# Order of work on VectorE and GpSimd in the attention loop of a two-layer decoder step

## The chip, the cores and the metric

One core of one Trainium2 chip runs the whole program. The metric is the device time of one execution in microseconds. Before the change the median of three runs is 1964.24 us (1963.74 to 1965.5).

The engines are named as the profile names them: PE (TensorE, with PEld for its weight loads), DVE (VectorE), ACT (ScalarE), POOL (GpSimd) and SP (SyncE, which issues most of the transfers).

## The reference

Two layers over 1024 prompt tokens and 8 sample tokens, model width 1024, all in float32. Layer 0 mixes with a gated recurrent block, layer 1 with sliding-window attention; a squared-ReLU MLP follows each. The change is inside the attention of layer 1, for the prompt tokens:

```python
def sink_attention(q, k, v, dist, mask, sinks):
    s = jnp.einsum('...qkgd,...skd->...kgqs', q, k).astype(jnp.float32) * (HEAD_DIM ** -0.5)
    s = s - alibi_slopes()[:, :, None, None] * dist.astype(jnp.float32)
    s = jnp.where(mask, s, NEG_INF)
    sink = sinks.astype(jnp.float32).reshape(N_KV, GROUP)[:, :, None, None]
    m = jnp.maximum(jnp.max(s, axis=-1, keepdims=True), sink)
    e = jnp.exp(s - m)
    p = e / (jnp.sum(e, axis=-1, keepdims=True) + jnp.exp(sink - m))
    return jnp.einsum('...kgqs,...skd->...qkgd', p.astype(v.dtype), v)
```

Queries come in 8 blocks of 128; each block sees its own block of keys and the one before it, and of these exactly 128 keys per query (window 128). There are 16 heads of width 64, in 4 groups that share keys and values.

## The kernel before, in words

The attention loop runs over 32 steps `g`: four groups of four heads (a pair of query tiles `t`, `t + 1`) times 8 query blocks `b`. Every query has 128 valid keys out of 256, and the kernel packs them into one 128-wide row: for key column j it takes the score of the older block or of the newer one, whichever is in the window. A step has three stages.

- `stage_a(g)` makes the probabilities. TensorE makes scores against both key blocks into a two-bank PSUM tile `bSS` (L1031), of which there is one. GpSimd meanwhile writes the distance bias into the step's `se` slot (L1034, L1036). VectorE then copies, under a mask, the older block's scores over the newer ones (L1038, only where there is an older block, so 28 times), adds the bias (L1039, the sum), takes the maximum (L1040) and a scaled negative of it (L1041). ScalarE takes four exponentials with row sums (L1044), VectorE the reciprocals (L1046), GpSimd scales by them (L1048).
- `stage_b(g)` transposes the four probability blocks on TensorE into the PSUM tile `bT` (L1058), of which there is one bank. ScalarE copies the result into the right half of `pt` (L1060), VectorE multiplies it by the mask of the newer block into the left half (L1062, the mask product). GpSimd subtracts the newer block's values from the older block's (L1056, the value difference) into one of four slots `dvs`.
- `stage_c(g0)` serves two steps at once. For each of them it multiplies values by the ScalarE half of `pt`, then value differences by the VectorE half (L1078, into the one bank `bO`), so that the mix of both value blocks comes out; ScalarE and VectorE split the result into two parts (L1085, L1086), and it is stored to DRAM (L1089) or kept.

In step `g` of the loop the scores of step g + 2, the transposes of step g and, every second time, the products of steps g - 2 and g - 1 are emitted. Between them TensorE gets matmuls of other work: first the query projections of the later heads (L938, with their own followers on ScalarE and VectorE: squares L877, a rounded part L879 and the remainder L880, and the transfers of both on SyncE, L886 and L887), and from step 22 on the output projection (L244), which needs the attention outputs loaded back (L1183) and the weights `w_out` (loaded by SyncE, L177, split by ScalarE L183 and VectorE L184). Each pair of query tiles has factors from its norms (L893 to L908, with L310 to L315), which bias, maximum and exponentials of the group need.

What sets the order: TensorE's instructions stay in the order in which they are written, because `pinned()` ties each to the one before it. On the other engines a scheduler of the framework orders the instructions when the program is built, by what is ready in its own estimate and by priority, which is the order of emission unless `tc.high_priority()` raises it. The order that comes out is a fixed queue for each engine: on the chip an instruction that waits holds everything behind it on that engine.

Of the kernel before, what the change touches and what calls it, by code (L numbers as in the profile page):

```python
# [13 lines left out]
ALU = mybir.AluOpType  # L14
PSUM = bass.MemoryType.PSUM

P = 128
# [9 lines left out]
NB = SEQ // P  # L27
# [38 lines left out]
def trunk(ctx: ExitStack, tc: tile.TileContext, I, O):  # L66
    nc = tc.nc
    pe, act, dve, pool, sp = nc.tensor, nc.scalar, nc.vector, nc.gpsimd, nc.sync
# [39 lines left out]
    def W(s="w"):  # L108
        return wp.tile([P, T], F32, tag="W", name=nm(s))
# [8 lines left out]
    def B(tag=None):  # L118
        if tag is None:
            tag = ring[turn[0] % len(ring)]  # L120
            turn[0] += 1
        return psum["pool"].tile([P, 512], F32, tag=tag, bufs=BANKS[tag], name=nm("b" + tag))


    def SB():
        return psum["pool"].tile([P, 1024], F32, tag="SS", bufs=1, name=nm("bSS"))
# [13 lines left out]
    def r_(x):  # L140
        return x.bitcast(F32R)
# [687 lines left out]
    def attention(hs):  # L829
# [123 lines left out]
        def vblk(b, p):  # L953
            h = b // 4
            o = (b % 4) * 256 + p * P
            return v_tiles[h][:, o:o + P]
# [34 lines left out]
        newer, newer_t = side_of[:, 0:P], side_of[:, P:2 * P]  # L991
        se2 = [W("se"), W("se")]
        ses = [x[:, o:o + 516].rearrange("p (x k) -> p x k", x=4) for x, o in ((se2[0], 0), (se2[0], 516), (se2[1], 0))]
        dvs = [se2[1][:, 516 + o:516 + o + P] for o in range(0, 4 * P, P)]
# [8 lines left out]
        def four(x):  # L1003
            return x.unsqueeze(1).to_broadcast([P, 4, P])

        def by_head(x):
            return x.rearrange("p (u t) -> p u t", u=2)
# [12 lines left out]
        def stage_a(g):  # L1020
            t, b = STEPS[g]
            p, i = divmod(t, 4)
            se, dn, s = ses[g % 3], den[g % 3], SB()
            f = fac[:, t % 4:t % 4 + 2, :, b, :]
            f0, f1 = [f[:, :, n, :].rearrange("p t u -> p u t") for n in range(2)]
            old, new = [s.rearrange("p (x h k) -> p x h k", x=4, h=2)[:, :, n, :] for n in range(2)]
            k0, n = ((b - 1) * P, 2 * P) if b else (0, P)
            for x in range(4):
                u, v = divmod(x, 2)
                for a, y in enumerate(kst[p][u]):  # L1030
                    pe.matmul(s[:, x * 256 + 256 - n:x * 256 + 256], lhsT=r_(qs[t + v][u][:, b * P:b * P + P]),  # L1031
                              rhs=r_(y[:, k0:k0 + n]), start=(a == 0), stop=(a == 1))
                h = (2 * p + u) * 4 + i + v
                pool.tensor_scalar(se[:, x, 0:P], dist if b else dist0, f[:, v, 1, u:u + 1], -SLOPES[h], ALU.mult, ALU.mult)  # L1034
                yield
            pool.tensor_tensor(by_head(se[:, :, P]), sinks[:, p, :, i:i + 2], f1, ALU.mult)  # L1036
            if b:
                dve.copy_predicated(new, four(newer.bitcast(mybir.dt.int32)), old)  # L1038
            dve.tensor_tensor(se[:, :, 0:P], new, se[:, :, 0:P], ALU.add)  # L1039
            dve.tensor_reduce(dn[:, 0:4], se, axis=mybir.AxisListType.X, op=ALU.max)  # L1040
            dve.scalar_tensor_tensor(by_head(dn[:, 4:8]), by_head(dn[:, 0:4]), -1.0, f0, ALU.mult, ALU.mult)  # L1041
            for x in range(4):
                u, v = divmod(x, 2)
                act.activation(se[:, x, :], se[:, x, :], AF.Exp, scale=f[:, v, 0, u:u + 1],  # L1044
                               bias=dn[:, 4 + x:5 + x], accum_out=dn[:, 8 + x:9 + x])
            dve.reciprocal(dn[:, 8:12], dn[:, 8:12])  # L1046
            for x in range(4):
                pool.tensor_scalar(se[:, x, 0:P], se[:, x, 0:P], dn[:, 8 + x:9 + x], 0.0, ALU.mult, ALU.add)  # L1048
            yield

        def stage_b(g):
            t, b = STEPS[g]
            se, pt = ses[g % 3], B("T")
            y = live["pt", g] = W("pt")
            if b:
                pool.tensor_tensor(dvs[g % 4], vblk(b - 1, t // 4), vblk(b, t // 4), ALU.subtract)  # L1056
            for x in range(4):
                pe.transpose(pt[:, x * P:x * P + P], se[:, x, 0:P], ident)  # L1058
                yield
            act.copy(y[:, 512:1024], pt)  # L1060
            if b:
                dve.tensor_tensor(y[:, 0:512].rearrange("p (x k) -> p x k", x=4), pt.rearrange("p (x k) -> p x k", x=4),  # L1062
                                  four(newer_t), ALU.mult)
            yield
# [162 lines left out]
        with pinned():  # L1227
            for g in range(AHEAD):
                ready(g)
                run(stage_a(g))  # L1230
                upto(41 + 6 * g)
        def scores(g):
            if g < NG:
                ready(g)
                run(stage_a(g))

        for g in range(NG):
            table = FILL if g < G0 else EARLY
            place = {0: 2, 1: 1}.get((g + AHEAD) % NB, 0)
            with pinned():  # L1240
                if place == 0:
                    scores(g + AHEAD)
                if g != G0:
                    upto(int(pace(table, g + 1 / 3)))
                if g and g % 2 == 0:
                    stage_c(g - 2)
                if g == G0:
                    run(fill)
                    taken[0], fill = 0, steps
                if place == 1:  # L1250
                    scores(g + AHEAD)
                upto(int(pace(table, g + 2 / 3)))
                run(stage_b(g))
                upto(int(pace(table, g + 1)))
                if place == 2:
                    scores(g + AHEAD)
# [373 lines left out]
```

## Time and profile before

| | |
|---|---|
| median of three runs | 1964.24 us (1963.74 to 1965.5) |
| the profiled execution | 1962.05 us |
| its span on the core | 1960.3 us |
| mean granted clock of TensorE | 0.996 |
| TensorE busy, whole span | 1945.4 us (99%) |
| VectorE busy, whole span | 1481.4 us (76%) |
| ScalarE busy, whole span | 1008.5 us (51%) |
| GpSimd busy, whole span | 367.8 us (19%) |
| attention loop | about 1040 to 1240 us of the span |

The span runs from the first to the last instruction of the profiled execution; its time is a little longer. A row of the timeline has the start in us, the duration in us, the engine, the line of the kernel, the operation, what is written and read, how many are merged, and in brackets the engine's idle time just before, with what ended it. A row of a window has the stretch, its length, then the busy time (and count) of PE, PEld, DVE, ACT and POOL, the granted clock, the DMA share and GB/s. "PE bSS L1031 <- DVE se L1039: 4.3, 2, 3.5" means that TensorE at line 1031 waited for VectorE's line 1039 for 4.3 us in all, twice, at most 3.5 us.

### The profile page before, as it was taken

The numbers are of one execution on the slowest core, as the hardware profiler recorded it, in microseconds if no ns is written. First come the engines' busy times: TensorE is split into PE (matmuls) and PEld (weight loads), VectorE is DVE, ScalarE is ACT, GpSimd is POOL, SyncE is SP. The second block draws the span as 40 slices with busy tenths as digits, with TensorE's granted clock in tenths as the row PEclk, the third lists the DMA queues.
The fourth block names the chain that finished last, engine by engine and source line by source line (L and its number), as shares of the span: only waits on it lengthen the run. The fifth ranks groups of instructions, "written<-read, shape, count | busy, mean of one in ns | idle before, by whom it ended". The sixth has DMA issues, their size and how long they took to land.

```text
span 1960.3 us, 34219 instructions
## 1 busy us (share of the span) xinstructions
PE 1945.4 (99%) x12844; PEld 1812.2 (92%) x12844; DVE 1481.4 (76%) x2711; ACT 1008.5 (51%) x1993; POOL 367.8 (19%) x702
## 2 busy tenths in 40 slices
PE   9999999999999999999999999999999999999999
PEld 8999999999999899999999887999999999999998
DVE  8896737987777878778743777579877779687784
ACT  6476635543434555445554676555443436455552
POOL 2330000000000232331032666000000003223321
PEclk9999999999999999999999999999999999999999
DMA  5111242244445788888452345612444447788877
GB/s 184 44 44 54 70 165 83 109 152 157 141 157 177 229 224 236 220 202 206 130 155 81 110 112 191 210 65 103 158 144 150 148 172 263 210 201 216 233 201 181
DMA packets 115909, 308.17 MB, mean 157 GB/s; under 512 B 17560, under 2 KB 46240, under 8 KB 115744
## 3 DMA queue, kind: packets, MB, share of 16 engines
q0 software_dynamic: 30720, 104.18, 22.1%
q1 hardware_dynamic: 54496, 129.36, 20.1%
q10 hardware_dynamic: 30528, 72.45, 10.3%
q8 instruction: 101, 1.65, 0.3%
q14 instruction: 64, 0.52, 0.1%
HBM read 178.08 MB, written 115.16 MB: 150 GB/s over the span
## 4 chain that ended last, share of the span: by engine, by line
PE 92%; DVE 3%; ACT 2%; DMA 1%; issue 1%; POOL 1%; SPq 0%; DVEq 0%; ACTq 0%
PE bD L609 36%; PE bZ L609 26%; PE bP L244 11%; PE bS L244 7%; PE bT L244 3%; PE bP L938 3%; PE bSS L1031 1%; PE bO L1078 1%; PE bS L968 1%; PE bT L1058 1%; DMA x<-xT 1%; ACT se L1044 0%; DVE wl L184 0%; DMA raw<-w_out 0%; DVE sq L295 0%
## 5 line engine op out<-in xcount | busy, mean ns | idle before, releaser
L609 PEld LDWEIGHTS bD<-op,op 128*128 128x128 f32 x3072 | 380.5, 188 | 7.9
L609 PE MATMUL bD<-op,op 128*128 128x260 f32 x3072 | 383.0, 282 | 0.0
L609 PEld LDWEIGHTS bD<-tl,op 128*128 128x128 f32 x2880 | 362.4, 188 | 11.6 <-DVE ho L757 0.3
L609 PE MATMUL bD<-tl,op 128*128 128x260 f32 x2880 | 366.4, 282 | 0.1
L622 POOL DMA_DIRECT2D tl<-hsum x210 | 125.4, 682 | 886.9 <-PE bD L609 785.4
L456 ACT CAST op<-ws 128x512 fp32r<-128x512 f32 (+2 forms) x288 | 158.7, 561 | 246.9 <-DVE ws L577 114.8
L609 PE MATMUL bZ<-op,op 128*128 128x512 f32 x1152 | 282.2, 394 | 0.0
L609 PE MATMUL bZ<-tl,op 128*128 128x512 f32 x1080 | 271.8, 394 | 0.2 <-DVE tl L464 0.2
L609 PEld LDWEIGHTS bZ<-op,op 128*128 128x128 f32 x1152 | 210.4, 188 | 43.6 <-ACT he L743 0.2
L609 PEld LDWEIGHTS bZ<-tl,op 128*128 128x128 f32 x1080 | 194.4, 188 | 37.7 <-DVE tl L464 0.7
L464 DVE TENSOR_TENSOR tl<-tl 128x520 fp32r<-128x520 f32 (+1 forms) x210 | 136.4, 692 | 77.1 <-ACT tl L463 76.9
L456 ACT CAST op<-raw 128x512 fp32r<-128x512 f32 (+2 forms) x216 | 120.9, 562 | 133.9 <-PE bD L609 73.0
L457 DVE TENSOR_TENSOR op<-ws,op 128x512 fp32r<-128x512 f32 (+2 forms) x288 | 171.5, 610 | 7.3 <-ACT op L456 7.1
L457 DVE TENSOR_TENSOR op<-raw,op 128x512 fp32r<-128x512 f32 (+2 forms) x216 | 131.7, 611 | 9.3 <-ACT op L456 8.5
L757 DVE TENSOR_TENSOR ho<-bD,ho 128x520 f32<-128x520 f32 x140 | 97.5, 697 | 37.1 <-PE bD L609 36.2
L463 ACT CAST tl<-tl 128x520 fp32r<-128x520 f32 (+1 forms) x210 | 117.5, 626 | 2.1 <-DVE ho L674 0.7
L184 DVE TENSOR_TENSOR wl<-raw,wh 128x512 fp32r<-128x512 f32 (+1 forms) x73 | 63.6, 890 | 34.7 <-ACT wh L183 18.1
L747 DVE TENSOR_TENSOR ho<-bZ,ho 128x512 f32<-128x512 f32 x72 | 49.6, 689 | 44.2 <-PE bZ L609 44.0
L731 ACT COPY he<-bZ 128x512 f32<-128x512 f32 x72 | 42.0, 583 | 75.3 <-PE bZ L609 69.8
L757 DVE TENSOR_TENSOR he<-bD,he 128x520 f32<-128x520 f32 x71 | 49.4, 696 | 40.6 <-PE bD L609 40.3
L749 ACT COPY he<-bZ 128x512 f32<-128x512 f32 x68 | 39.9, 587 | 77.0 <-PE bZ L609 64.9
L183 ACT CAST wh<-raw 128x512 fp32r<-128x512 f32 (+1 forms) x76 | 57.2, 775 | 36.2 <-PE bT L244 11.3
(371 smaller groups left out, 3839.4 us busy)
## 6 DMA issues: line engine op xcount, KB each, us to landing
raw<-w_up SPq DMA_DIRECT2D x64, 512.0 KB, 3.8
tl<-hsum POOLq DMA_DIRECT2D x120, 260.0 KB, 6.7
raw<-w_dn SPq DMA_DIRECT2D x64, 384.0 KB, 6.2
tl<-hsum POOLq DMA_DIRECT2D x90, 256.0 KB, 6.3
spill<-ho POOLq DMA_DIRECT2D x32, 516.0 KB, 6.9
spill<-he POOLq DMA_DIRECT2D x32, 516.0 KB, 6.3
hsum<-ts ACTq DMA_DIRECT2D x30, 520.0 KB, 4.0
hsum<-ho ACTq DMA_DIRECT2D x30, 516.0 KB, 3.5
```

The source lines that it names most:

```text
L183: act.copy(r_(hi[:, sl]), raw[:, sl])
L184: eng.tensor_tensor(r_(lo[:, sl]), raw[:, sl], hi[:, sl], ALU.subtract)
L244: pe.matmul(o, lhsT=r_(wt[:, col(k):col(k) + P]), rhs=r_(xt[:, cs(c)]), start=(k == first and a == 0), stop=(k == final and a == 2))
L456: act.copy(r_(hi), x)
L457: dve.tensor_tensor(r_(lo), x, hi, ALU.subtract)
L463: act.copy(r_(hi), lo)
L464: eng.tensor_tensor(r_(lo), lo, hi, ALU.subtract)
L609: pe.matmul(d[:, 512 * b:512 * b + c], lhsT=r_(wt[:, j * P:j * P + P]), rhs=r_(xt[:, c * b:c * b + c]), start=first and j == 0 and a == 0, ...
L622: pool.dma_start(t[:, n:2 * n], src)
L747: dve.tensor_tensor(o0, d, o[:, HP], ALU.add)
L757: last["sum"] = dve.tensor_tensor(t, inner(d), t, ALU.add).ins
L938: pe.matmul(o, lhsT=r_(wt[:, k * P:k * P + P]), rhs=r_(xt[:, cs(c)]), start=(k == 0 and a == 0), stop=(k == M8 - 1 and a == 2))
```

## The change

Two edits. In `stage_a` the masked copy and the sum are emitted with high priority. In `stage_b` the value difference is emitted behind the transposes and for the next step: step g makes the difference that step g + 1 will use, in the slot `(g + 1) % 4`. The number of value differences is the same (28), and so are all other instructions.

```diff
             pool.tensor_tensor(by_head(se[:, :, P]), sinks[:, p, :, i:i + 2], f1, ALU.mult)
-            if b:
-                dve.copy_predicated(new, four(newer.bitcast(mybir.dt.int32)), old)
-            dve.tensor_tensor(se[:, :, 0:P], new, se[:, :, 0:P], ALU.add)
+            with tc.high_priority():
+                if b:
+                    dve.copy_predicated(new, four(newer.bitcast(mybir.dt.int32)), old)
+                dve.tensor_tensor(se[:, :, 0:P], new, se[:, :, 0:P], ALU.add)
             dve.tensor_reduce(dn[:, 0:4], se, axis=mybir.AxisListType.X, op=ALU.max)
...
             y = live["pt", g] = W("pt")
-            if b:
-                pool.tensor_tensor(dvs[g % 4], vblk(b - 1, t // 4), vblk(b, t // 4), ALU.subtract)
             for x in range(4):
                 pe.transpose(pt[:, x * P:x * P + P], se[:, x, 0:P], ident)
                 yield
+            if (g + 1) % NB:
+                pool.tensor_tensor(dvs[(g + 1) % 4], vblk(b, t // 4), vblk(b + 1, t // 4), ALU.subtract)
             act.copy(y[:, 512:1024], pt)
```

The edit adds one line, so in the rows of the changed kernel the copy is L1039, the sum L1040, the maximum L1041, the exponentials L1045, the reciprocals L1047, ScalarE's copy L1061, the mask product L1063, the split L1086 and L1087, and the load of outputs L1184. Tile names carry a number that counts tiles (`pt1595`) and one that differs between builds.

TensorE's order is the same in both. The orders of the other engines differ in the attention loop alone. Three places follow.

VectorE around the scores of step 13 (`bSS1599`; `pt1595` is the mask product of the step whose transposes stand in `bT1594`). Before:

```order
L1046 RECIPROCAL den0_10399<-den0_10399 128x4
L1038 COPY_PREDICATED bSS1599_12334<-side1344_10405,bSS1599_12334 128x4x128
L1086 TENSOR_TENSOR o1593_12298<-bO1589_12284,o1592_12297 128x256
L1062 TENSOR_TENSOR pt1595_12310<-bT1594_12309,side1344_10405 128x512
L880 TENSOR_TENSOR lo1597_12320<-bP1585_12229,hi1596_12319 128x344
L1039 TENSOR_TENSOR se1345_10407<-bSS1599_12334,se1345_10407 128x4x128
```

and of the change:

```order
L1039 COPY_PREDICATED bSS1599_12335<-side1344_10405,bSS1599_12335 128x4x128
L1047 RECIPROCAL den0_10399<-den0_10399 128x4
L1087 TENSOR_TENSOR o1593_12299<-bO1589_12285,o1592_12298 128x256
L1040 TENSOR_TENSOR se1345_10407<-bSS1599_12335,se1345_10407 128x4x128
L1063 TENSOR_TENSOR pt1595_12311<-bT1594_12310,side1344_10405 128x512
L880 TENSOR_TENSOR lo1597_12321<-bP1585_12230,hi1596_12320 128x344
```

The copy has passed a reciprocal, and the sum has passed the mask product and L880.

VectorE, and below it ScalarE, two steps later around `pt1630` (`den0` belongs to the exponentials of step 15; `hi1626` and `lo1627` are the two parts of a query projection). VectorE before, then of the change:

```order
L907 TENSOR_SCALAR st_330<-r1619_12525 128x16
L1062 TENSOR_TENSOR pt1630_12554<-bT1629_12553,side1344_10405 128x512
L908 RECIPROCAL st_330<-st_330 128x16
L1046 RECIPROCAL den0_10399<-den0_10399 128x4
L880 TENSOR_TENSOR lo1627_12542<-bP1608_12434,hi1626_12541 128x344
```

```order
L907 TENSOR_SCALAR st_330<-r1619_12526 128x16
L908 RECIPROCAL st_330<-st_330 128x16
L1047 RECIPROCAL den0_10399<-den0_10399 128x4
L880 TENSOR_TENSOR lo1627_12543<-bP1608_12435,hi1626_12542 128x344
L1063 TENSOR_TENSOR pt1630_12555<-bT1629_12554,side1344_10405 128x512
```

ScalarE at the same place, before and of the change:

```order
L312 ACTIVATE q1622_12529<-r01621_12528 128x16
L1060 COPY pt1630_12554<-bT1629_12553 128x512
L1044 ACTIVATE se1345_10407,den0_10399<-se1345_10407,den0_10399,st_330 128x129 x4
L879 CAST hi1626_12541<-bP1608_12434 128x344
L1085 CAST o1632_12580<-bO1631_12571 128x256
```

```order
L312 ACTIVATE q1622_12530<-r01621_12529 128x16
L1045 ACTIVATE se1345_10407,den0_10399<-se1345_10407,den0_10399,st_330 128x129 x4
L879 CAST hi1626_12542<-bP1608_12435 128x344
L1061 COPY pt1630_12555<-bT1629_12554 128x512
L1086 CAST o1632_12581<-bO1631_12572 128x256
```

Both halves of `pt1630` now stand behind the exponentials of step 15 and the parts of the query projection.

SyncE ahead of the output projection (loads of attention outputs and pieces of a query tile), before and of the change:

```order
L1183 DMA oh1702_13134<-od0h_10409 128x344 x2
L886 DMA q01671_12899<-hi1683_13009 64x344
L887 DMA q01671_12899<-lo1684_13010 64x344
L886 DMA q11672_12900<-hi1683_13009 64x344
L887 DMA q11672_12900<-lo1684_13010 64x344
L1183 DMA ol1703_13135<-od0l_10410 128x344
```

```order
L1184 DMA oh1702_13135<-od0h_10409 128x344 x2
L1184 DMA oh1702_13135<-od0h_10409 128x336
L1184 DMA ol1703_13136<-od0l_10410 128x344
L1184 DMA oh1704_13139<-od1h_10411 128x344
L1184 DMA ol1705_13140<-od1l_10412 128x344
L886 DMA q01671_12900<-hi1683_13010 64x344
```

Four loads now go out ahead of the four q pieces. Around them the order of the loads is the same, except that the last parts of some come a little earlier.

## Prediction

> **What bounds the kernel now.** I read the page first, then the busy time of the attention loop, then TensorE's waits in that loop.
>
> ```profile
> PE 1945.4 (99%) x12844; PEld 1812.2 (92%) x12844; DVE 1481.4 (76%) x2711; ACT 1008.5 (51%) x1993; POOL 367.8 (19%) x702
> ...
> 1040.00:1240.00 200.00, 193.75 (x1381) 169.23 (x1379) 134.97 (x321) 126.62 (x419) 115.06 (x316) 0.98 0.46 136
> ...
> PE bSS L1031 <- DVE se L1039: 4.3, 2, 3.5
> PE bO L1078 <- DVE pt L1062: 1.3, 1, 1.3
> ```
>
> The first row is the whole execution: TensorE is busy 99% of the 1960.3 us. The second is the stretch from 1040 to 1240 us, which holds the attention loop (span, then busy time of PE, PEld, DVE, ACT and POOL, the granted clock, the DMA share and GB/s). VectorE works 135 of 200 us there, so it has room, and TensorE lacks only 200 - 193.75 = 6.25 us. The last two rows say what TensorE waited for: 4.3 + 1.3 = 5.6 of those 6.25 us, in three waits. So a change on VectorE can gain at most about 6 us of idleness here, and whatever makes a wait for TensorE is paid in full, because TensorE has no slack to catch up with.
>
> Neither edit touches TensorE's own order, which is pinned. The question is therefore which instruction TensorE finds unfinished at each of its places.
>
> ```profile
> L1039 DVE TENSOR_TENSOR se<-bSS,se 128x512 f32<-128x512 f32 x32 | 22.0, 688 | 3.0 <-POOL se L1034 1.4
> L1038 DVE COPY_PREDICATED bSS<-side,bSS 128x512 f32<-128x512 int32 x28 | 19.4, 692 | 6.8 <-PE bSS L1031 6.5
> L1062 DVE TENSOR_TENSOR pt<-bT,side 128x512 f32<-128x512 f32 x28 | 19.2, 687 | 4.3 <-ACT pt L1060 3.9
> L1060 ACT COPY pt<-bT 128x512 f32<-128x512 f32 x32 | 18.7, 584 | 16.4 <-PE bT L1058 15.3 <-DVE o L1086 1.0
> L1056 POOL TENSOR_TENSOR se<-vt 128x128 f32<-128x128 f32 x24 | 11.2, 470 | 10.8 <-PE bO L1078 10.8
> ```
>
> Columns: instructions of one kind in the loop, busy time and mean ns, then the engine's idle time before them and what ended it.
>
> **The change part by part.** Nothing is added or removed: the same 28 masked copies (L1038, 0.69 us each), 32 sums (L1039, 0.69 us), 28 mask products (L1062, 0.69 us) and 28 value differences. What changes is who goes first. (I use the line numbers of before.)
>
> Value differences: the 24 plain ones take 11.2 us on GpSimd and wait 10.8 us for TensorE's L1078, which must have read the slot. No row shows TensorE waiting for L1056, so making them earlier gains nothing at L1078. Their cost is bounded above by one 0.47 us place on GpSimd ahead of a bias (L1034) that a sum waits for (1.4 us in all, the L1039 row) and below by nothing. I take 0, since GpSimd is busy only 115 of 200 us.
>
> Priority, place one: the sum of step 13 moves ahead of the mask product of the older step, pt1595.
>
> ```profile
> 1130.36 0.18 DVE L1046 RECIPROCAL den<-den 128x4 f32<-128x4 f32 x1 [2.54 <-ACT se L1044]
> 1130.45 0.67 DVE L1038 COPY_PREDICATED bSS<-side,bSS 128x512 f32<-128x512 int32 x1
> 1131.04 0.41 DVE L1086 TENSOR_TENSOR o<-bO,o 128x256 fp32r<-128x256 f32 x1
> 1131.36 0.68 DVE L1062 TENSOR_TENSOR pt<-bT,side 128x512 f32<-128x512 f32 x1
> ...
> 1132.38 0.68 DVE L1039 TENSOR_TENSOR se<-bSS,se 128x512 f32<-128x512 f32 x1
> ...
> 1130.71 1.43 POOL L1048 TENSOR_SCALAR se<-se,den 128x128 f32<-128x128 f32 x4
> ...
> 1132.19 0.63 PE L1058 MATMUL bT<-con,se 128*128 128x128 f32 x4
> ```
>
> The transposes of the next step (PE at 1132.19) need the one bT bank, which the mask product reads until 1131.36 + 0.68 = 1132.04. TensorE is there just behind it. With the sum in between, the mask product starts one sum later: successive VectorE instructions of 0.68 us start 0.60 apart, so +0.60. Against that, the copy no longer waits for the reciprocal and may start up to 0.09 earlier. The same transposes also need GpSimd's scaling (1130.71 + 1.43 = 1132.14), which starts behind the reciprocal; with the copy ahead of the reciprocal it too moves by about 0.55. So nothing that ends last here escapes: 0.5 to 0.6 us of new wait, and I take 0.6. The sum being 1 us earlier gains nothing, since no row shows TensorE waiting for it here.
>
> Priority, place two: step 15's exponentials get ahead of the copy of pt1630 on ScalarE, and its reciprocal and the q remainder L880 ahead of pt1630's mask product on VectorE.
>
> ```profile
> 1143.97 0.57 ACT L1060 COPY pt<-bT 128x512 f32<-128x512 f32 x1
> 1144.43 0.50 ACT L1044 ACTIVATE se<-se,den,st 128x129 f32<-128x129 f32 x1
> ...
> 1146.36 0.42 ACT L879 CAST hi<-bP 128x344 fp32r<-128x344 f32 x1
> ...
> 1144.76 0.68 DVE L1062 TENSOR_TENSOR pt<-bT,side 128x512 f32<-128x512 f32 x1
> ...
> 1146.82 0.52 DVE L880 TENSOR_TENSOR lo<-bP,hi 128x344 fp32r<-128x344 f32 x1 [0.15 <-ACT hi L879]
> ...
> 1146.05 0.60 PE L1078 MATMUL bO<-pt,vt 128*64 128x256 f32 x4
> 1146.48 0.60 PE L1078 MATMUL bO<-pt,se 128*64 128x256 f32 x4
> ...
> 1151.80 0.39 PE L1031 MATMUL bSS<-kh,q 128*128 128x256 f32 x1 [0.84 <-DVE se L1039]
> ```
>
> Before, the copy ends at 1143.97 + 0.57 = 1144.54 and the mask product at 1145.44, 1.5 and 1.0 us ahead of the products that read them (1146.05 and 1146.48). Now the four exponentials (1144.43 to 1146.36, 1.93 us) and the cast (0.42) stand first. With the 0.6 us of place one, the exponentials start near 1144.6, the cast ends near 1146.95 and the copy near 1147.45; L880 ends near 1147.4, and the mask product near 1148.1. TensorE would come to the first product at 1146.65 and waits until about 1147.5 (0.85); its second half comes 0.43 later, at 1147.95, and waits until about 1148.2 (0.25). Place two costs 1.1 us. The least is 0.5 (the exponentials 0.3 earlier than I place them, and the mask product not last: 0.85 - 0.3), the most 1.6 (each of the exponentials' end, cast, copy and L880 another 0.15 late, the pause that the L880 row shows, rounded down). What is late next is the step behind: the 0.84 us wait of 1151.8 hangs on this same stage's result and moves with it.
>
> Place three: the end of the loop, where step 21's sum passes pt1678's mask product, and SyncE's loads of attention outputs pass four q pieces.
>
> ```profile
> 1172.87 0.68 DVE L1062 TENSOR_TENSOR pt<-bT,side 128x512 f32<-128x512 f32 x1
> 1173.47 0.68 DVE L1039 TENSOR_TENSOR se<-bSS,se 128x512 f32<-128x512 f32 x1
> ...
> 1173.70 0.63 PE L1058 MATMUL bT<-con,se 128*128 128x128 f32 x4
> ...
> 1175.67 0.47 SPq L886 DMA_DIRECT2D q<-hi  x1
> 1185.12 0.53 SPq L177 DMA_DIRECT2D raw<-w_out  x1
> ...
> 1189.69 0.23 ACT L312 ACTIVATE q<-r 128x16 f32<-128x16 f32 x1
> 1191.06 1.14 ACT L183 CAST wh<-raw 128x512 fp32r<-128x512 f32 x2 [1.14 <-DMA raw<-w_out]
> ...
> 1190.50 0.43 DVE L313 SCALAR_TENSOR_TENSOR q<-qs,st,q 128x16 f32<-128x16 f32 x1
> ...
> 1195.16 0.58 PE L1031 MATMUL bSS<-kh,q 128*128 128x256 f32 x1 [3.47 <-DVE se L1039]
> ...
> q<-lo SPq DMA_DIRECT2D x7, 86.0 KB, 2.2
> oh<-od0h SPq DMA_DIRECT2D x2, 172.0 KB, 2.4
> ...
> 1186.00:1188.00 2.00, 1.03 (x8) 0.64 (x9) 1.95 (x4) 1.91 (x8) 0.28 (x1) 1.00 1.14 299
> ```
>
> The swap at 1172.87 repeats place one: 0.60 us on the transposes at 1173.70, kept through the 1.3 us wait at L1078, whose mask product moves too. But soon after comes the wait of 3.47 us, which ends by a chain of its own: the weights w_out land (issued 1185.12, cast at 1191.06), VectorE splits them, and only behind that come the q factors, the bias and the sum. Time lost just before that wait is given back if its end does not move. Four loads of about 172 KB now go out ahead of the q pieces that SyncE issued from 1175.67, before the busy stretch (DMA share 1.14 and 299 GB/s at 1186), and four q pieces of 86 KB go later, so some 0.35 to 0.5 MB less stands before w_out; at 299 GB/s that is 1.2 to 1.7 us, less a later issue of up to 0.6. The landing can come earlier only until L312 (1189.69 + 0.23, plus 0.6) and L313 (1190.50 + 0.43, plus 0.6) become the last: the end of the wait moves by -0.5 to +0.7 us. I take 0: landing earlier and L313 later about cancel, and the 0.6 us of this place disappears in the wait.
>
> Sum: 0 + 0.6 + 1.1 + 0 = **+1.7 us** on the profiled execution's 1962.05 (span 1960.3), which lies 2.19 us under the median of 1964.24; on the median that is **1965.9**. By the bounds, 0.5 + 0.5 - 0.5 to 0.6 + 1.6 + 0.7: +0.5 to +2.9, so 1964.7 to 1967.1 for this case.
>
> **The rivals.** *Clock, two ways.* The clock row has a price of its own.
>
> ```profile
> 1194.00:1196.00 2.00, 0.84 (x4) 0.84 (x5) 1.45 (x3) 0.26 (x1) 1.62 (x6) 0.58 1.00 395
> 1196.00:1198.00 2.00, 2.00 (x10) 1.94 (x10) 0.80 (x2) 2.00 (x8) 0.00 (x0) 0.50 1.04 356
> 1200.00:1202.00 2.00, 2.00 (x13) 2.00 (x12) 1.85 (x5) 0.82 (x4) 1.91 (x6) 0.71 1.03 386
> ...
> 1282.00:1284.00 2.00, 2.00 (x10) 2.00 (x9) 0.52 (x1) 0.31 (x1) 0.00 (x0) 0.50 0.00 0
> ```
>
> After the 3.47 us wait the granted clock is 0.50 until about 1201: six microseconds at half rate, some 2.7 us lost. After the 1.3 us wait it stayed at full rate. The clock also fell at 1280 to 1286, with TensorE busy throughout, so idleness is not its only cause.
>
> (A) Faster side: w_out lands early enough that the 3.47 us wait shrinks towards 2.7, and the clock stays up. Then 1.7 - 2.7 = -1.0: 1963.2. For it: the lighter queue. Against it: 2.7 is still twice the wait that kept the clock.
>
> [...]
>
> (B) Slower side: at place two TensorE waits long enough for the clock to fall there. Mechanism: copy, cast and exponentials on ScalarE are serial, so one more late exponential chain (1.93 us) ahead of the copy brings the wait from 1.1 to 3.0. It decides from somewhere between 1.3 us (clock kept) and 3.47 us (clock fell). Price: 1.7 + 1.9 + 2.7 = +6.3, 1970.5; with the clock alone 1.7 + 2.7 = +4.4, 1968.6.
>
> (C) The change does nothing: the mask products are not last, because the 0.6 us of places one and three vanish in the 3.47 us wait and, at place two, the exponentials are ready only after the copy's operand, so that the copy loses less than the 1.5 us it has in hand. Then 1964.2. Against it: the exponentials alone last 1.93 us, and the copy now stands behind them on one engine.
>
> (D) The waits that VectorE ended go: the 0.84 us one of 1151.8 with place two's order, and the 3.47 with its clock. -4.3 - 2.7 + 1.7 = -5.3: 1958.9. Against it: the sums that end them wait for GpSimd's bias or for the mask product, and neither is overtaken at those two places.
>
> **How the numbers follow.** Forecast 0.60, (A) 0.13, (B) 0.11, (C) 0.13, (D) 0.03. About 0.2% (3.9 us, so 1960.3 to 1968.2) is what a measurement of this kernel can tell from no change. Faster by that much is (D) and little else: 0.04. Slower is (B) with the forecast's upper tail: 0.12. The same: 0.84. The range takes in (A) and (C) and stops short of (B): 1962.8 to 1968.2.
>
> **What would show it.** Right: TensorE's waits name L1058 or PEld for about 0.6 us near 1132 and 1174, and L1078 for about 1.1 us near 1147 behind ScalarE's copy; the 0.84 stays; the wait of 3.47 is shorter by about 0.6. Wrong: no wait at L1078 near 1147 (place two), the granted clock under 1.00 near 1150 (then B) or at 1.00 after 1195 (then A), or the loop's TensorE idleness below 6.25 us.

## The result, and the profile after

| | before | changed |
|---|---|---|
| median of 20 runs each, side by side | 1963.9 us | 1966.68 us |
| ratio, with its 95% interval | | 1.0014 (1.0008 to 1.0021) |
| profiled execution, span | 1960.3 us | 1963.9 us |

The change costs 0.14%, by the interval 1.6 to 4.1 us: little, but clearly above zero. The forecast was +1.7 us and 1965.9. In the experiments below one execution, of the kernel with the value differences alone, was a slow one of 6225.28 us, and its ratio leaves it out.

TensorE's busy time hardly moves; its waits in the loop do. First the whole span and the loop window of the changed kernel, then all waits of TensorE from 1040 to 1260 us (us in total, times, longest). Lines are those of the changed kernel: the transposes are L1057, the products L1079.

```profile
PE 1946.1 (99%) x12844; PEld 1811.2 (92%) x12844; DVE 1481.1 (75%) x2711; ACT 1007.9 (51%) x1993; POOL 366.5 (19%) x702
...
1040.00:1240.00 200.00, 191.30 (x1368) 166.55 (x1368) 132.60 (x317) 125.02 (x417) 113.54 (x316) 0.99 0.46 135
...
PE bSS L1031 <- DVE se L1040: 4.5, 3, 3.4
PE bO L1079 <- DVE pt L1063: 1.4, 1, 1.4
PE bN L898 <- ACT qc L895: 1.0, 2, 0.7
PE bO L1079 <- ACT pt L1061: 0.6, 1, 0.6
PE bT L1057 <- POOL se L1049: 0.6, 1, 0.6
PE bT L1057 <- DVE pt L1063: 0.5, 1, 0.5
```

Before, the same view had 4.3, 1.3 and 0.3 us. Those three are still there. New are 0.26 us at the scores near 1109, 0.7 us at L898 and three waits of 0.5 to 0.6 us for the copy and the mask product of the transposes, or for the scaling that stands beside it. These are the rows, in order of time; the waits of 0.81 and 3.40 us among them were there before (0.84 and 3.47):

```profile
1109.77 0.38 PE L1031 MATMUL bSS<-kh,q 128*128 128x256 f32 x1 [0.26 <-DVE se L1040]
...
1132.98 0.63 PE L1057 MATMUL bT<-con,se 128*128 128x128 f32 x4 [0.57 <-POOL se L1049]
...
1143.68 0.44 PE L898 MATMUL bN<-con,qc 128*128 128x128 f32 x2 [0.71 <-ACT qc L895]
...
1148.56 0.65 PE L1079 MATMUL bO<-pt,vt 128*64 128x256 f32 x4 [0.61 <-ACT pt L1061]
1149.28 0.65 PE L1079 MATMUL bO<-pt,se 128*64 128x256 f32 x4
...
1154.62 0.39 PE L1031 MATMUL bSS<-kh,q 128*128 128x256 f32 x1 [0.81 <-DVE se L1040]
...
1177.09 0.63 PE L1057 MATMUL bT<-con,se 128*128 128x128 f32 x4 [0.52 <-DVE pt L1063]
...
1198.47 0.44 PE L1031 MATMUL bSS<-kh,q 128*128 128x256 f32 x1 [3.40 <-DVE se L1040]
```

TensorE issues the same instructions in the same order in both kernels, so each can be paired with itself and its two start times subtracted. This tells more than the sum of the waits, since pauses under 0.2 us have no bracket in the rows. The lateness of the changed kernel grows at these instructions and nowhere else by more than 0.2 us:

| start before | what | later by | added there |
|---|---|---|---|
| up to 1109 | before the loop's new order begins | 0.15 | 0.15 |
| 1109.47 | scores L1031 | 0.30 | +0.15 |
| 1132.19 | transposes (place one) | 0.79 | +0.49 |
| 1142.02 | L898, q factors | 1.66 | +0.87 |
| 1146.05, 1146.48 | products (place two) | 2.80 | +0.85, +0.29 |
| 1173.70 | transposes (place three) | 3.39 | +0.59 |
| 1195.16 | end of the 3.47 us wait | 3.31 | -0.08 |
| 1195 to 1201 | TensorE at half clock | 2.15 | about -1.1 |
| 1279 to 1287 | TensorE at half clock | 3.68 | +1.5 |

The last two rows are the clock: it was granted at 0.50 for 6.83 us at each of these places before, and for 3.41 and 10.24 us in the changed kernel. They are taken up at the end. Without them the loop costs 3.1 to 3.2 us more.

### The profile page after: what moved, and what is told of

It reads as the page before. It is cut to its first block, busy times and chain, and to the rows that moved or that the text cites. A ratio compares the mean times of both kernels' runs of the same rounds, so it can differ in the third digit from the quotient of the medians.

```text
span 1963.9 us, 34221 instructions
## 1 busy us (share of the span) xinstructions
PE 1946.1 (99%) x12844; PEld 1811.2 (92%) x12844; DVE 1481.1 (75%) x2711; ACT 1007.9 (51%) x1993; POOL 366.5 (19%) x702
## 4 chain that ended last, share of the span: by engine, by line
PE 92%; DVE 3%; ACT 2%; DMA 2%; issue 1%; POOL 0%; ACTq 0%; SPq 0%; DVEq 0%; POOLq 0%
PE bD L609 36%; PE bZ L609 26%; PE bP L244 12%; PE bS L244 7%; PE bT L244 3%; PE bP L938 3%; PE bSS L1031 1%; PE bO L1079 1%; PE bS L968 1%; DMA tl<-hsum 1%; PE bT L1057 1%; ACT se L1045 0%; DVE wl L184 0%; DVE sq L295 0%; DMA raw<-w_out 0%
```

## The experiments

All ratios are against the kernel before, run beside the other on the same chip; each kernel has 11 or 12 runs, the kernel before 21 to 35.

**Each edit alone.** The priority alone:

```diff
+            with tc.high_priority():
                 if b:
                     dve.copy_predicated(new, four(newer.bitcast(mybir.dt.int32)), old)
                 dve.tensor_tensor(se[:, :, 0:P], new, se[:, :, 0:P], ALU.add)
```

> The kernel before with the priority of masked copy and sum alone; the value differences stay where they were. VectorE's, ScalarE's and SyncE's orders are those of the changed kernel. Theory (the priority is the whole loss): TensorE has the changed kernel's new waits, 0.3 us near 1109, 0.6 near 1132, 0.7 near 1143, 0.6 near 1148 and 0.5 near 1177, its loop waits add up to about 8.6 us, and the time is +1.6 to +4.1 us as for the whole change. Rival (GpSimd's new order takes part, since the wait of 0.57 us near 1133 is put down to GpSimd's scaling): that wait is below 0.3 us and the time rises by less than 1.5 us.

Ratio 1.0013 (1.0005 to 1.0022): the whole loss. Its waits are those of the changed kernel one by one, the one put down to GpSimd's scaling included (0.57 us near 1133). The rival is out: GpSimd's new order plays no part that these runs show.

```profile
PE bSS L1031 <- DVE se L1040: 4.5, 3, 3.4
PE bO L1079 <- DVE pt L1063: 1.4, 1, 1.4
PE bN L898 <- ACT qc L895: 1.2, 2, 0.9
PE bO L1079 <- ACT pt L1061: 0.6, 1, 0.6
PE bT L1059 <- POOL se L1049: 0.6, 1, 0.6
PE bT L1059 <- DVE pt L1063: 0.5, 1, 0.5
```

The value differences one step ahead, alone:

```diff
-            if b:
-                pool.tensor_tensor(dvs[g % 4], vblk(b - 1, t // 4), vblk(b, t // 4), ALU.subtract)
...
+            if (g + 1) % NB:
+                pool.tensor_tensor(dvs[(g + 1) % 4], vblk(b, t // 4), vblk(b + 1, t // 4), ALU.subtract)
```

> The kernel before with the value differences one step ahead alone; only GpSimd's order differs from before. Theory: nothing moves; TensorE's waits in the loop are the three of before (0.8, 1.3 and 3.5 us) and the time is within 1 us of before. Rival (the difference in the new place holds up a scaling or a bias on GpSimd): a new wait at the transposes or at the scores of 0.3 us or more, +1 us or more. A gain would show as a wait of before that is shorter by over 0.3 us.

Ratio 0.9999 (0.999 to 1.0008), and TensorE waits where it waited before:

```profile
PE bSS L1031 <- DVE se L1039: 3.8, 2, 3.0
PE bO L1078 <- DVE pt L1062: 1.3, 1, 1.3
PE bN L898 <- ACT qc L895: 0.3, 1, 0.3
```

Nothing new, and nothing gained that can be measured. The longest wait is 0.46 us shorter in this one profile, because the w_out load was cast 5.53 us after its issue (1184.54 to 1190.07) and not 5.94; the runs show no gain from it.

**Which steps.** Priority in one step of the 32, and in all but that one:

```diff
+            with tc.high_priority() if g == 13 else nullcontext():
```

> The kernel before with priority in step 13 alone (value differences as before). On VectorE and ScalarE this changes places one and two and nothing else; on SyncE it puts one w_out load behind one store. Theory: the waits of 0.57, 0.7 and 0.6 + 0.3 us near 1133, 1143 and 1148 all appear, those near 1109 and 1177 do not; TensorE is 2.4 to 2.6 us later at the 0.84 us wait near 1152, and the time is +2 to +3 us. Rival (the sum of many small places, or the clock, makes the loss): under +1 us, and no wait at the products near 1148.

> The kernel before with priority in every step except 13 (value differences as before). Of the three places only the third changes, with the small moves near 1091 to 1109. Theory: the waits of 0.57 us at the transposes near 1133 and of 0.6 us at the products near 1148 are gone, the one of 0.5 us near 1177 is there, and it is mostly given back at the wait of 3.47 us (3.0 to 3.5): the time is within 1 us of before. Rival (place three and the changed loads carry a good part of the loss): +1.5 us or more.

Step 13 alone: 1.0010 (1.0002 to 1.0019), about +2.0 us. All but 13: 1.0000 (0.9991 to 1.0009). So, as far as 11 runs can tell (the first interval reaches from 0.4 to 3.7 us), one of 32 sums carries the loss, by what it passes and by what its earlier exponentials pass. In the profile of step 13 alone the waits near 1133 and 1148 are there (0.57 and 0.62 us, at 1136.16 and 1150.79), the one near 1177 is not, and the one at L898 is not either, though it was expected. By pairing, places one and two cost 0.44 and 1.09 us in it. It also holds what the expectation did not have, a wait of 1.92 us near 1111 behind a long store issue, with 3.4 us at half clock after it, until about 1115.4 (a matmul of 344 columns took 0.49 us there, before and after it 0.32). How many of the 11 runs have that is not known, so about 1.5 of the 2.0 us are traced to what the sum passes, and the rest is open. In the profile of all but 13 only place three is left, beside 0.26 us near 1109, and its 0.5 us is given back at the long wait (2.87 instead of 3.47 us):

```profile
PE bSS L1031 <- DVE se L1040: 4.0, 3, 2.9
PE bO L1079 <- DVE pt L1063: 1.4, 1, 1.4
PE bT L1059 <- DVE pt L1063: 0.5, 1, 0.5
PE bN L898 <- ACT qc L895: 0.3, 1, 0.3
```

**Is being passed the cause?** The changed kernel, with the same priority for what was passed:

```diff
+            with tc.high_priority():
                 act.copy(y[:, 512:1024], pt)
                 if b:
                     dve.tensor_tensor(y[:, 0:512].rearrange("p (x k) -> p x k", x=4), pt.rearrange("p (x k) -> p x k", x=4),
                                       four(newer_t), ALU.mult)
```

> The changed kernel with the same high priority on ScalarE's copy and VectorE's mask product of the transposes (L1061, L1063), so that neither is passed by a sum, an exponential or a query remainder at places one to three. Theory (being passed is what costs): the waits near 1133, 1148 and 1177 are gone, the 0.8, 1.3 and 3.5 us waits stay, and the time is that of before, within 1 us, that is 2 to 3 us under the changed kernel. Rival (something else in the change costs): one of the three waits stays with 0.4 us or more, and the time stays at +1.5 us or more.

All three new waits are gone, and the 1.3 us one with them. The wait at L898 near 1076 grew from 0.26 to 0.73 us, behind the raised copy:

```profile
PE bSS L1031 <- DVE se L1040: 6.4, 3, 5.5
PE bN L898 <- ACT qc L895: 0.7, 1, 0.7
```

The ratio is 1.0005 (0.9996 to 1.0014), so not told from no change, and at its upper end not from the changed kernel either: that being passed makes the three waits is shown by the rows, and the time alone does not show it. The expectation missed one thing: the long wait did not stay at 3.5 us, it grew to 5.48, since its end hangs on the w_out load, issued at 1185.18 and cast at 1191.35 as before, while TensorE reached it 1.45 us sooner; the last q factors also stand behind that split there. What is won ahead of it is lost in it.

**The wait at L898.** In the changed kernel ScalarE stood in the issue of one store for 1.99 us (the same store took 0.41 before), right behind SyncE's issue of a 512 KB load, and L895 was queued behind it. First three rows of ScalarE in the changed kernel, then two of step 13 alone, where a store at another place took 2.16 us with no such load near it:

```profile
1140.70 0.33 ACTq L1090 DMA_DIRECT2D od3h<-o  x1
1141.16 1.99 ACTq L1090 DMA_DIRECT2D od3l<-o  x1
1143.25 0.37 ACT L895 COPY qc<-bN 128x256 f32<-128x256 f32 x1 [2.10 <-DVE bSS L1039]
```

```profile
1106.46 0.33 ACTq L1090 DMA_DIRECT2D od1h<-o  x1
1106.92 2.16 ACTq L1090 DMA_DIRECT2D od1l<-o  x1
```

All stores issued by SyncE instead:

```diff
-                        (act if u else sp).dma_start(d[:, dst], y)
+                        sp.dma_start(d[:, dst], y)
```

> The changed kernel with all stores of attention outputs issued by SyncE, so that ScalarE issues no transfer in the loop. In the changed kernel the issue of one store held ScalarE for 1.99 us instead of 0.35 near 1141, and TensorE waited 0.71 us behind it. Theory (a long issue on ScalarE is chance, and what it costs is ScalarE's time): the wait of 0.7 us at L898 near 1143 is gone, and no wait of a similar kind appears near 1110; the waits near 1133 and 1148 stay; the time is 0.5 to 1.5 us under the changed kernel, +1 to +2 us against before. Rival (ScalarE is late there for the priority's sake): the wait near 1143 stays with 0.4 us or more.

The wait near 1143 is gone, no other of its kind appears, and the waits near 1133 and 1148 stay (0.57 and 0.62 us); the one of place three is 0.80 us here, near 1176. The ratio is 1.0007 (0.9998 to 1.0016): between before and the changed kernel, as expected, but the interval reaches both. One store still took 1.32 us to issue, now on SyncE behind the same load, and one near 1107 took 1.80; no wait of TensorE stands right behind either. That the issue itself is long at times is shown; what decides when is not. In step 13 alone the store came 0.27 us behind the load, as in the changed kernel (0.26), and took 0.36.

**The long wait.** The split of a w_out unit is called one step later, so that VectorE's queue has the last q factors ahead of it:

```diff
-            if 20 <= g < 24:
-                ensure(index["wo1", g - 20])
+            if g in (20, 21, 23, 24):
+                ensure(index["wo1", g - 20 - (g > 21)])
```

> The kernel before, with the splitting of the third and fourth w_out unit called one step later, so that on VectorE the last q factors stand ahead of that split. Theory (the wait of 3.47 us is the w_out landing that VectorE's queue puts ahead of the q factors): the wait shrinks to about 1.6 us and, if so short a wait keeps the clock up, the time falls by 1.8 + 2.7 = 4.5 us; with the clock still down by 1.8. Rival (the scores wait for the factors themselves or for GpSimd's bias): the wait stays above 3 us and the time within 1 us.

The wait fell from 3.47 to 1.94 us, as the theory says, but the time did not (0.9998, 0.9988 to 1.0007): the clock still fell after 1.94 us (0.83 from 1194 to 1204 us), and this profile has a wait of 1.29 us near 1111 behind a 1.53 us store issue, at a place where the kernel before waits 0.13 us. With priority for the last q factors besides:

> The kernel with the late w_out split, and priority for the last q factors: one swap on VectorE and one on ScalarE bring the factors 0.4 to 0.8 us forward. Theory: the wait of 1.9 us there shrinks to 1.1 to 1.5 us; if that keeps the clock up after it, the time is 3 to 5 us under before, if not 1.5 to 2.5. Rival (the clock falls whatever the wait, or the time lost moves to the output projection): the clock is still at 0.5 for 3 us or more after it, and the time within 1 us of before.

1.79 us, with a mean granted clock of 0.998 in the profiled run, and the ratio is 0.9996 (0.9988 to 1.0005). The factors came forward by less than hoped.

**A version that beats both.** The mask product's priority wins 1.3 us ahead of the long wait and loses it there; the late split shortens the long wait. Together, with and without the change's two edits:

> The changed kernel with the mask product's priority, the late w_out split and the last q factors first, together. Theory: the waits near 1133, 1148 and 1177 are gone (from the mask product's priority), the 1.3 us wait too, and the wait of 3.5 us (5.5 with the mask product's priority alone) becomes 1.5 to 2.5, since the w_out landing no longer stands ahead of the factors: TensorE's waits in the loop add up to 3 to 4.5 us instead of 5.9 before and 8.5 in the changed kernel, and the time is 1 to 4 us under before, 4 to 6 under the changed kernel. Rival (what is gained at one wait is lost at the next, as with the late split alone): waits of 5 us or more in all, and the time within 1 us of before.

> The same without the change's two edits: the kernel before with priority for copy and mask product of the transposes, the late split and the last q factors first. Theory (priority for masked copy and sum is worth nothing to TensorE even where it passes no mask product): within 1 us of the run with the edits, 1 to 4 us under before. Rival (the sum's priority gains once the mask product is safe): 1.5 us or more above the run with the edits.

Both take 0.9983 of the time before (0.9975 to 0.9992, and 0.9974 to 0.9992): 3.0 and 2.9 us less than before, and so some 5 to 6 less than the changed kernel, which was not run beside them. The first, with the edits:

```profile
1040.00:1240.00 200.00, 194.60 (x1408) 170.41 (x1407) 135.03 (x326) 126.68 (x421) 115.24 (x316) 1.00 0.48 141
...
PE bSS L1032 <- DVE se L1041: 4.3, 4, 2.6
PE bN L898 <- ACT qc L895: 0.7, 1, 0.7
PE bSS L1032 <- DVE den L1048: 0.3, 1, 0.3
```

The waits are 5.3 us and not the 3 to 4.5 that were expected, mainly because the long one is still 2.57. That is only 0.6 us less than the 5.9 of before, so the waits do not account for a gain of 3.0. Part of it may be the clock: what the mean granted clock of the runs lacks to 1.00, times their length, is 5.2 us with the edits, 6.1 without and 7.2 before. By this estimate 1 to 2 us of the gain are clock; where the rest comes from is open. The two versions differ by 0.1 us: even where the sum passes no mask product, its priority is worth nothing that these runs show (their intervals are over 3 us wide).

## Why the prediction was right, and where it was not

**The direction and the waits of the three places were right; the size was 1.1 us short, and the give-back at the long wait was wrong.** +1.7 us was forecast, +2.8 measured (1.6 to 4.1). In the profile two more waits, which the prediction did not name, come to 1.0 us.

- *Value differences, 0:* right, by the run with them alone.
- *Place one, 0.6 us:* 0.49 by pairing. It ended on GpSimd's scaling (1132.92), the second chain that was named there; the mask product ended 0.09 us earlier.
- *Place two, 1.1 us (0.85 at the first product, 0.25 at the second):* 0.85 and 0.29. The order of the end was as written: the exponentials from 1145.69 on, the cast at 1147.60, the copy at 1147.93, and TensorE at 1148.56. The 0.84 us wait behind it stayed (0.81).
- *Place three, 0.6 us on the transposes:* 0.59.
- *Place three, given back at the long wait so that the sum is 0:* wrong. The end of that wait came 3.31 us later, with 3.39 at the transposes ahead of it, so 0.1 us was given back, not 0.6. The step that failed is that "some 0.35 to 0.5 MB less stands before w_out", so that the load lands earlier. SyncE's queue shows it:

```profile
1175.09 1.41 SPq L1184 DMA_DIRECT2D oh<-od0h  x3
1179.49 0.32 SPq L1184 DMA_DIRECT2D ol<-od0l  x1
1179.91 0.38 SPq L1184 DMA_DIRECT2D oh<-od1h  x1
1180.38 0.38 SPq L1184 DMA_DIRECT2D ol<-od1l  x1
1180.96 1.11 SPq L886 DMA_DIRECT2D q<-hi  x2
1182.16 1.19 SPq L887 DMA_DIRECT2D q<-lo  x2
...
1188.60 0.53 SPq L177 DMA_DIRECT2D raw<-w_out  x1
1194.38 1.14 ACT L183 CAST wh<-raw 128x512 fp32r<-128x512 f32 x2 [1.08 <-DMA raw<-w_out]
```

Three loads went out early, but the fourth waited until 1179.49, 3 us after the third. SyncE's waits name TensorE's query projection (L938) for 3.1 us of it. The q pieces behind it went out from 1180.96, and all of them still ahead of the w_out load: between the first of these loads and w_out stand the same six q pieces as before, and 14 loads of outputs where 13 stood. Nothing was taken out of its way. The w_out load was issued 11.51 us after the transposes of place three began, where it was 11.42: it does not follow a chain of its own, but moves with TensorE, and the end of the wait moved with it (used 5.78 us after the issue, where it was 5.94).

In the run with all steps but 13, 0.5 us was given back. The load was issued just as long after the transposes there (11.51 us), but used 5.27 us after its issue, 0.67 less than before. Three profiles with the old order of loads have 5.34, 5.53 and 5.94 us, so whether the new order makes the load land earlier is not shown.

- *Missed:* 0.15 us at 1109, where the reciprocal and the q remainder go ahead of other work, and 0.87 at L898. Neither stands in the prediction. At L898 SyncE's issue of a w_out load has come behind a store of its own (1140.90, before 1139.04), and the long store issue on ScalarE follows right behind it. It came in two profiles with this swap (0.7 and 0.9 us of wait) and not in a third, so on average the change pays less than 0.9 us for it.

Sum of the forecast terms with their measured sizes: 0.49 + 1.14 + 0.59 - 0.08 = 2.1, and 1.0 of missed terms, 3.1 to 3.2 us in this profile; the runs say 2.8. That these agree is in part luck. The clock, which the forecast left out of its sum, has a share in the 2.8: what the mean granted clock of the runs lacks to 1.00, times their length, is 7.8 us for the changed kernel (20 runs), and 6.6 to 7.2 us for the kernel before (three sets of 21 to 35 runs). By this estimate some 0.6 to 1.2 us are clock, and the new waits cost less on average than in this profile.

**The rivals.** (A), the long wait shrinking and the clock staying up, did not happen in the changed kernel (3.40 us), but did in the run with all but 13 (2.87 us, clock at 1.00), so it is a real path of this loop. Its bound was wrong: 2.7 us is not too long for the clock to stay up, as it was 1.00 after a wait of 2.87 us there, though it fell at one of 1.94 us in the late split. Nor did it bring what (A) promised: that kernel takes 1.0000 of the time before. (B) did not come: place two, 1.14 us in all, left the clock at 1.00 there. (C) is out: TensorE waited at all three places, and the waits of the first two did not vanish. (D) did not happen.

## What to carry to other kernels

Ask whether the engine that bounds the loop waits for an operation before giving that operation priority. Here TensorE waited for the sum at two places before, and at the longer one the sum itself was waiting, for GpSimd's bias (0.95 us, L1034). Where there is nothing to gain, priority can only cost: look at what it passes, and at what the passed one feeds. Follow a raised instruction to the next engine too; the dearest swap here was not on VectorE but on ScalarE, where exponentials that became ready earlier passed a copy. Where a transfer sets the end of a later wait, what is won or lost ahead of it is partly paid back there, and of the kernels tried here only those that moved both took less time.

## What the hardware did that was not expected

**The clock was at 0.50 for 3.4 to 10.2 us at a time.** Between 1190 and 1300 us the granted clock was 0.50 for 6.83 us from 1194.33 and for 6.83 us from 1279.66 before, for 3.41 us from 1198.67 and for 10.24 us from 1280.59 in the changed kernel, and 1.00 in the rest. At half rate 3.41, 6.83 and 10.24 us lose 1.71, 3.41 and 5.12 us of TensorE's work. Rows of before, of the changed kernel, of all steps but 13 and of the late split (10 and 14 us long; the granted clock is third from the end):

```profile
1194.00:1204.00 10.00, 8.84 (x47) 8.19 (x49) 7.82 (x15) 5.68 (x19) 5.62 (x16) 0.66 1.04 383
1278.00:1292.00 14.00, 14.00 (x74) 14.00 (x74) 6.94 (x31) 4.43 (x14) 0.00 (x0) 0.76 0.07 26
```

```profile
1194.00:1204.00 10.00, 6.60 (x37) 6.26 (x37) 6.75 (x15) 4.79 (x13) 4.43 (x15) 0.83 1.05 385
1278.00:1292.00 14.00, 14.00 (x69) 14.00 (x70) 7.44 (x33) 4.98 (x15) 0.00 (x0) 0.63 0.06 21
```

```profile
1194.00:1204.00 10.00, 9.31 (x67) 7.99 (x68) 8.71 (x19) 6.92 (x24) 6.91 (x21) 1.00 1.00 377
```

```profile
1194.00:1204.00 10.00, 8.33 (x51) 7.24 (x51) 7.63 (x17) 5.45 (x19) 6.25 (x18) 0.83 1.01 384
```

0.34 of 10 us is 6.83 us at half clock, 0.17 is 3.41; 0.24 of 14 us is 6.83, 0.37 is 10.24. The changed kernel happened to lose 1.7 us less after its long wait and 1.7 us more near 1280, so the clock nearly cancels in the pair of profiles above.

By the length of TensorE's wait: in the profiles of before, of the changed kernel, of each edit alone, of step 13 alone and of all but 13, the clock fell at none of the waits up to 1.37 us. It fell at those of 1.92 us (step 13 alone), 1.94 us (the late split) and 2.83 us (step 13 alone), but not at those of 2.57 us (the mask product's priority and the late split, with the edits), 2.6 us (the same without them) and 2.87 us (all but 13), with 1.00 from 1194 to 1204 us after each. It fell at the long waits of 3.01 us (the value differences alone), 3.40 us (the changed kernel), 3.45 us (the priority alone) and 3.47 us (before). For step 13 alone and each edit alone, and for all but 13 outside of 1194 to 1204 us, this is read from matmuls of 344 columns, which start 0.29 us apart at a clock of 0.50 and 0.16 us apart at 1.00 in the profile of before. So between 1.92 and 2.87 us the length does not decide, and what does is not shown.

Near 1280 the clock fell with TensorE busy throughout, 14.00 of 14 us in the rows of before and of the changed kernel. It fell near there in the profiles of each edit alone, of step 13 alone, of all but 13, and of the mask product's priority and the late split without the edits too; with the edits it was 1.00 from 1278 to 1292 us. Before, twenty matmuls of 8 columns (2.40 us, from 1275.79) stand just ahead; what decides at this place is open.

The clock goes with the spread of the runs too (1959.56 to 1966.98 us before): in 35 other runs of the same kernel, time and granted clock have a correlation of -0.82.

**A store's issue held its engine for 1.1 to 2.2 us at times,** instead of 0.33 to 0.50. Of the eleven profiles with stores on ScalarE, eight have one such issue (1.14 to 2.21 us) in the loop, near 1107 or near 1141, always the second store of a pair; before, the value differences alone and all steps but 13 have none on ScalarE. What stood behind it waited (in the changed kernel ScalarE was idle for 2.10 us ahead of L895), and TensorE lost 0.2 to 1.9 us each time. In most of them the order near 1107 is that of before, so the order of that place alone does not decide it.
